# Attention scores that VectorE writes from PSUM into the probabilities' tiles, with new instruction orders for three engines

## The chip, the core and the metric

The kernel runs on one core of one Trainium2 chip. A core has TensorE (PE in the profile; its weight loads are listed apart as PEld), VectorE (DVE), ScalarE (ACT), GpSimd (POOL) and the queue SyncE (SP), which here only issues transfers. The metric is the device time of one execution in microseconds, the median over several.

## The reference

One layer of a streaming encoder on 1024 frames of width 1024, all in float32: a norm and one wide projection; eight heads of "forgetting" attention; eight heads of attention in a band; both mixed under gates; an output projection; a feed-forward block; a last norm. The change lies in the attention:

```
# forgetting heads: causal, the logits get the summed log forget gates
sc = einsum('bhqd,bhkd->bhqk', qi, k) * scale + ci[..., None] - c[:, :, None, :]
sc = where(key_pos <= tq, sc, NEG)
# band heads: own chunk of 64 and the eight before it, and a bias by distance
sc = where(valid, einsum('bhqd,bhkd->bhqk', qi, kb) * scale + bias, NEG)
# both
p = softmax(sc); out = einsum('bhqk,bhkd->bhqd', p, v)
```

## The kernel before

Everything outside the attention is dense products in units of a Strassen scheme: float32 operands are split into a high and a low half, and each product is three matmuls of 128 rows by 512 columns. Around the attention, a gate projection runs ahead of it and the rest of the branch products behind it.

The 16 heads are worked off one after the other, the eight forgetting heads first (`HEADS`, pairs 4 to 7), then the eight band heads. A head has eight blocks of 128 queries. Block i of a forgetting head meets i+1 blocks of keys, so 36 in all; in a band head at most five, so 30. The steps of a head have letters:

- S (`make_scores`, `score`): TensorE makes a block's scores, in two terms (operand `qk` of 128 rows, `sk` of 96), in a PSUM tile `s` of 1024 columns. There are two such tiles.
- R (`take_lowest`, `lowest`): VectorE adds the mask (`wide`) or the band's bias (`bc`), takes the negative, writes that back over the scores, and takes each row's minimum into `mn`; a second, short instruction reads the minimum out.
- E (`take_exp`, `soften`): ScalarE makes the exponential of the negative with `mn` as bias, which gives the probabilities `p`, and their sum in `den`. There is one tile `p` for each block index (tag `p0` to `p7`), so a head overwrites those of the head before.
- T (`turn`): TensorE transposes blocks of `p` into a PSUM tile `pt`, in groups of up to four (`key_groups`). A forgetting head has ten groups: three for the first four query blocks, seven for the last four. It rotates over three PSUM tiles, a band head over two.
- H (`round_p`): ScalarE rounds `pt` to the high half `th`. L (`low_p`): VectorE makes the rest, `tl`. Four tiles of each.
- P (`weigh_next`): TensorE multiplies `th` and `tl` with the values into one PSUM tile `pv`, for each half of the queries.
- V and X (`evacuate`, `evacuate_rest`): ScalarE, and for the second half VectorE, take `pv` out (`on`, `lo`, `mv`).
- F: a step of the branch product, three matmuls, as filling for TensorE in band heads from the tenth head on (`FILL_FROM = 9`); M takes its result out. W and O are weights and outputs for the branch product at the end.

The order is written out by hand. The strings `INTRO`, `FOX_HEAD`, `BAND_HEAD` and `LAST_HEAD` list the letters of a head; each engine keeps the order of its own letters (`Ordered`). T, H, L, P of a string belong to its own head, S, R, E to the head after it, since eight chunks of S, R and E are done ahead, between the steps of the last gate projection. `INTRO` is issued first and its letters are then taken out of the first string. A scheduler places the rest, outside of the attention, by itself.

A step waits for its data and for its buffer: S for the scores' tile of two chunks before, T for its `pt` tile, H and L for their tiles, the first P of a half for `pv`. Line 106 is the helper that issues every ordered instruction, so nearly all rows of the attention carry L106, and tiles tell them apart.

Of the kernel before, what the change touches and what calls it, by code (L numbers as in the profile page):

```python
# [18 lines left out]
P = 128  # L19
# [8 lines left out]
BAND = 640  # L28
# [10 lines left out]

HEADS = [(pr, hh) for pr in (4, 5, 6, 7, 0, 1, 2, 3) for hh in range(2)]  # L40
SK = HD + 32
INTRO = "TTTHHLHLPTHPLTLHPVTTH"
FOX_HEAD = "STTHRSETSHLRLREPTHLPTHESHLPVTRTELSRXHTLHSPEPHLTPTSHRLPEPHLRLESPRPVXE"
BAND_HEAD = "TTFSRHEFFHSLLFSMTHRPTPELFTFPRHLEHSVTLSFRXTHRPPELSTFHLERPHLESMPRPVESRXE"
LAST_HEAD = "FFFFMWTHTFFFLHFTPLTWPHMLFFWFFTHHLMLTPFFHLTVFXFHLPPMOOTHLOPPOPWVXOO"
FILL_FROM = 9

LEAD, XB, XR = 3, 4, 6

# [43 lines left out]
def hybrid_block(ctx: ExitStack, tc: tile.TileContext, xT, xN, g1, wall, wf, fb, relb, g2, g3, outT):  # L93
# [17 lines left out]
    def pool(stack, name, side, bufs=1, **kw):  # L111
        return stack.enter_context(tc.tile_pool(name=name, bufs=bufs, side=side, reuse_waits="tile", **kw))
# [366 lines left out]
    def load_head(n, eng):  # L479

        pr, hh = HEADS[n]
        e, p = 2 * pr + hh, apq[n % 2]
        qk = p.tile([P, 2, S], F32R, tag="qk", name=f"qk{n}")
        if n < 2:
            sks.append(p.tile([SK, 2, S], F32R, tag="sk", name=f"sk{n}"))
            G.memset(sks[n][HD:SK].bitcast(F32), 0.0)
            G.memset(sks[n][HD:HD + 3, 1, :].bitcast(F32), -1.0)
        sk = sks[n % 2]
        if pr >= 4:
            loads.append(eng.dma_start(sk[HD:HD + 3, 0, :].bitcast(F32), c3_dram[:, 2 * (pr - 4) + hh, :]).ins)  # L490
        elif n < 10:
            G.memset(sk[HD:SK, 0, :].bitcast(F32), 0.0)
        loads.append(eng.dma_start(qk.bitcast(F32), qk_dram[e]).ins)
        loads.append(eng.dma_start(sk[0:HD].bitcast(F32), sk_dram[e]).ins)
        operands[n] = (qk, sk)

    loads, sks, biases, operands, smalls, probs = [], [], {}, {}, {}, {}

    def score(n, i, bank, te):

        pr = HEADS[n][0]
        qk, sk = operands[n]
        j0, W = window(pr, i)
        off = P if W == BAND else 0
        spans = [(max(off, HALF * x), min(off + W, HALF * (x + 1))) for x in range(2 if off + W > HALF else 1)]
        rows = slice(i * P, (i + 1) * P)
        for t, w in enumerate((qk, sk)):
            for a, b in spans:
                keys = slice(j0 * P + a - off, j0 * P + b - off)
                te.matmul(bank[:, a:b], w[:, 1, rows], w[:, 0, keys], start=t == 0, stop=t == 1)  # L510

    def lowest(n, i, bank, ve):

        pr = HEADS[n][0]
# [151 lines left out]
    apq = [pool(astack, "apq0", "right")]  # L666
    app = pool(astack, "app", "right")
    load_head(0, G)
    chunks = [(n, i) for n in range(16) for i in range(8)]
    made, cut, spent = [], [], []  # L670

    def make_scores():
        if len(made) == len(chunks):
            return
        n, i = chunks[len(made)]
        made.append(pss.tile([P, S], F32, tag="s", name="s"))
        score(n, i, made[-1], TO)
        if i == 7 and 0 < n < 14:
            load_head(n + 2, LO)

    def take_lowest(ve=VO):
        if len(cut) < len(chunks):
            n, i = chunks[len(cut)]
            lowest(n, i, made[len(cut)], ve)
            cut.append(None)
            if i == 7 and n + 2 < 16:
                load_bias(n + 2, LO)

    def take_exp(ae=AO):
        if len(spent) < len(chunks):  # L690
            soften(*chunks[len(spent)], made[len(spent)], ae)
# [259 lines left out]
    def branch_weight():  # L951
# [6 lines left out]
        G.tensor_tensor(wl, raw, wh.bitcast(F32), op=ALU.subtract)  # L958

    acts = {"O": split_o, "W": branch_weight, "S": make_scores, "R": take_lowest, "E": take_exp, "T": turn, "H": round_p, "L": low_p, "P": weigh_next,  # L960
            "V": evacuate, "X": evacuate_rest, "F": filler, "M": gate_fill}
    heads = [t for n, (pr, hh) in enumerate(HEADS) for t in
             (FOX_HEAD if pr >= 4 else LAST_HEAD if n == 15 else BAND_HEAD if n >= FILL_FROM else
              BAND_HEAD.replace("F", "").replace("M", ""))]
    for t in INTRO:
        heads.remove(t)
    for t in chain(INTRO, heads):
        acts[t]()
        if t == "S" and len(made) in (8 * FILL_FROM - 4, 8 * FILL_FROM):
            next(fills)  # L970
# [376 lines left out]
```

## Time and profile before

| | us |
|---|---|
| median of 3 runs (lowest, highest) | 1427.55 (1426.97, 1428.85) |
| profiled execution | 1430.48 |
| its span, first to last instruction | 1428.5 |
| mean granted TensorE clock in it | 0.995 |
| attention, about | 400 to 665 of the span |

The span begins after some 2 us that belong to the execution and not to the profile. Times in rows of the trace count from the span's start. A group's row gives busy time, mean ns of one instruction, and the idle time before them with what ended it. In the view by windows each stretch lists its length, then PE, PEld, DVE, ACT and POOL busy with their numbers of instructions, the granted clock, the DMA share and GB/s.

### The profile page before, as it was taken

Reading aid. Unit: us, or ns where it says so; the run is one execution under the profiler, and the core shown is the slowest. Engines: PE = TensorE matmul, PEld = TensorE weight load, DVE = VectorE, ACT = ScalarE, POOL = GpSimd, SP = SyncE. Lnnn points to the kernel's source line nnn. Section 1 sums busy time; section 2 is a strip of 40 time slices with the busy share of each in tenths; the row PEclk is TensorE's granted clock in tenths of the full one; section 3 lists DMA queues with packets and bytes.
Section 4 is the critical chain, followed back from the end, with each engine's and each line's share of the span. In section 5 each row is a group of like instructions: output and inputs, shape, how many; then the busy total and the mean of one; then the engine's idle time right before and its main releaser. Section 6 shows DMA issues by size and latency. Waiting matters only on the chain.

```text
span 1428.5 us, 20411 instructions
## 1 busy us (share of the span) xinstructions
PE 1400.7 (98%) x6676; PEld 1168.7 (82%) x6676; DVE 885.1 (62%) x1389; ACT 706.6 (49%) x1361; POOL 812.2 (57%) x639
## 2 busy tenths in 40 slices
PE   9999999999999999999999999999999999999996
PEld 6788888888878888888888888888888888888885
DVE  7756445543258887776655855545555559998644
ACT  8534333343358887775454543333333444444653
POOL 0477777778832233113724677777777545567564
PEclk9999999999999999999999999999999999999998
DMA  8546667773454668886644244444444784678263
GB/s 282 154 116 194 187 196 219 204 198 121 147 169 147 185 209 248 246 257 215 213 162 146 68 166 151 155 154 157 148 154 169 252 269 156 178 234 225 81 221 118
DMA packets 132820, 259.75 MB, mean 182 GB/s; under 512 B 18594, under 2 KB 20642, under 8 KB 129642
## 3 DMA queue, kind: packets, MB, share of 16 engines
q1 hardware_dynamic: 84570, 172.79, 38.6%
q10 hardware_dynamic: 44944, 77.78, 17.2%
q0 software_dynamic: 3200, 7.88, 2.5%
q8 instruction: 52, 0.85, 0.2%
q14 instruction: 54, 0.44, 0.1%
HBM read 172.70 MB, written 85.69 MB: 181 GB/s over the span
## 4 chain that ended last, share of the span: by engine, by line
PE 87%; DVE 3%; issue 3%; ACT 2%; POOL 2%; DMA 2%; SPq 0%; POOLq 0%; ACTq 0%; DVEq 0%
PE u L216 44%; PE dS L216 12%; PE dA L216 5%; PE o L216 5%; PE s L106 5%; PE pv L106 4%; PE pt L106 3%; PE m L106 3%; PE m L216 3%; POOL wl_A L165 1%; PE u L106 1%; DMA xg<-xT 1%; DMA xT<-a_dram 1%; ACT p L106 1%; PE vtp L627 0%
## 5 line engine op out<-in xcount | busy, mean ns | idle before, releaser
L165 POOL TENSOR_TENSOR wl_A<-wr,wh_A 128x512 fp32r<-128x512 f32 x118 | 158.4, 1352 | 94.0 <-ACT wh_A L163 77.0
L165 POOL TENSOR_TENSOR wl_S<-S,wh_S 128x512 fp32r<-128x512 f32 x102 | 136.0, 1337 | 32.9 <-ACT wh_S L163 32.3
L163 ACT CAST wh_S<-S 128x512 fp32r<-128x512 f32 x105 | 64.6, 621 | 114.0 <-PE u L216 53.9
L163 ACT CAST wh_A<-wr 128x512 fp32r<-128x512 f32 x105 | 65.0, 620 | 88.7 <-PE u L216 55.8
L106 DVE TENSOR_TENSOR tl<-pt,th 128x512 fp32r<-128x512 f32 (+1 forms) x144 | 90.5, 641 | 25.9 <-ACT th L106 24.4
L165 POOL TENSOR_TENSOR wl_S<-ks,wh_S 128x512 fp32r<-128x512 f32 x48 | 69.1, 1501 | 53.4 <-ACT wh_S L106 50.0
L590 DVE TENSOR_TENSOR u<-u,u 128x512 f32<-128x512 f32 x70 | 48.8, 698 | 76.0 <-PE u L216 73.6
L106 ACT ACTIVATE p<-s,mn 128x640 f32<-128x640 f32 (+3 forms) x120 | 84.4, 703 | 16.6 <-DVE mn L106 15.5
L106 ACT CAST th<-pt 128x512 fp32r<-128x512 f32 (+1 forms) x144 | 77.6, 551 | 24.5 <-PE pt L106 22.3
L106 PE MATMUL pt<-ident,p 128*128 128x128 f32 x528 | 78.1, 274 | 1.2 <-DVE zt L403 1.1
L186 POOL TENSOR_TENSOR S<-wr,wr 128x512 f32<-128x512 f32 x35 | 46.3, 1324 | 54.8 <-DMA wr<-wall 50.2
L106 PEld LDWEIGHTS pt<-ident,p 128*128 128x128 f32 x528 | 62.2, 141 | 11.0 <-PE pv L106 2.0
L106 PE MATMUL s<-qk 128*128 128x384 f32 (+2 forms) x192 | 58.6, 360 | 8.1 <-ACT p L106 7.3
L165 POOL TENSOR_TENSOR wl_A<-ka,wh_A 128x512 fp32r<-128x512 f32 x32 | 45.1, 1419 | 35.6 <-ACT wh_A L106 34.1
L278 ACT CAST qkh<-qk 128x512 fp32r<-128x512 f32 x32 | 19.9, 621 | 87.5 <-DMA qk_dram<-qkl 34.2
L1102 ACT ACTIVATE v<-v 128x512 f32<-128x512 f32 x64 | 40.4, 632 | 45.1 <-DVE v L1101 42.9
L924 POOL TENSOR_TENSOR on<-on,lo 128x512 f32<-128x512 f32 x7 | 9.0, 1292 | 92.7 <-ACT lo L106 92.7
L106 PE MATMUL pv<-th,v 128*128 128x512 f32 (+3 forms) x180 | 61.3, 348 | 0.1
L583 DVE TENSOR_TENSOR u<-u,c 128x512 f32<-128x512 f32 x35 | 24.5, 699 | 59.4 <-PE u L216 57.3
L106 PE MATMUL pv<-tl,v 128*128 128x512 f32 (+3 forms) x180 | 56.8, 335 | 0.2 <-DVE tl L106 0.2
L1101 DVE SCALAR_TENSOR_TENSOR v<-u,rstd 128x512 f32<-128x512 f32 x64 | 43.9, 688 | 20.1 <-PE u L216 18.1
L581 DVE TENSOR_TENSOR c<-u,u 128x512 f32<-128x512 f32 x35 | 24.2, 691 | 50.7 <-PE u L216 48.9
(445 smaller groups left out, 4742.2 us busy)
## 6 DMA issues: line engine op xcount, KB each, us to landing
wr<-wall SPq DMA_DIRECT2D x233, 256.0 KB
a_dram<-at ACTq DMA_DIRECT2D x64, 256.0 KB
xT<-a_dram SPq DMA_DIRECT2D x64, 256.0 KB
qk<-qk_dram SPq DMA_DIRECT2D x15, 1024.0 KB
qk_dram<-qkh ACTq DMA_DIRECT2D x96, 128.0 KB
a_dram<-v ACTq DMA_DIRECT2D x48, 256.0 KB
xB<-a_dram SPq DMA_DIRECT2D x44, 256.0 KB
z_dram<-zt ACTq DMA_DIRECT2D x32, 256.0 KB
```

What stands on the lines that cost most here:

```text
L106: return lambda *a, **kw: tc.keep_in_program_order(getattr(self.eng, name)(*a, **kw))
L163: (act.tensor_copy if act is G or act is V else act.copy)(wh, src)
L165: lows.append(eng.tensor_tensor(wl, src, wh.bitcast(F32), op=ALU.subtract))
L186: eng.tensor_tensor(t, raw(3), raw(2), op=ALU.add)
L216: done = eng.matmul(bank, w[wi], x[xi], start=(first and t == 0), stop=(t == n - 1 and not part), skip_group_check=part or not first)
L278: A.copy(dst[0], src)
L581: V.tensor_tensor(c22, banks[2], u2, op=ALU.add)
L583: V.tensor_tensor(banks[1], banks[3], c22, op=ALU.add)
L590: V.tensor_tensor(banks[b], banks[b], u2, op=ALU.add)
L924: G.tensor_tensor(o, o, lows_o[pr], op=ALU.add)
L1101: V.scalar_tensor_tensor(v, src, 0.0, rstd[:, hs(h)], op0=ALU.max, op1=ALU.mult)
L1102: A.activation(v, v, AF.Square)
```

## The change

The minimum step writes the shifted scores into the probabilities' tile `p` in SBUF instead of back into PSUM, and the exponential works in place there. The PSUM tile `s` is so read by VectorE alone, and the tile `p` is taken by `lowest` instead of `soften`. The blocks of a head go in the order 0 to 5, 7, 6 instead of 0 to 7. The four strings are new; each has the same letters of each kind as before, save that `INTRO` now holds 24 letters instead of 21 (eight T instead of seven, two S and one R, which were not in it, one L more, one P less and no V).

```diff
-INTRO = "TTTHHLHLPTHPLTLHPVTTH"
-FOX_HEAD = "STTHRSETSHLRLREPTHLPTHESHLPVTRTELSRXHTLHSPEPHLTPTSHRLPEPHLRLESPRPVXE"
...
+INTRO = "TTTHHLTLHHLPTHLPLTTSSRHT"
+FOX_HEAD = "TTHHSSRSTRHLSLEPLTRETHHPLLPTVHRSTXLTSPRTHLSTRPEEHLREHEPSHLPLPPPREVXE"
...
+FOX_BLOCKS = (0, 1, 2, 3, 4, 5, 7, 6)
+BAND_BLOCKS = (0, 1, 2, 3, 4, 5, 7, 6)
...
         x = bank[:, off:off + W]
+        p = probs[n, i] = app.tile([P, (i + 1) * P], F32, tag=f"p{i}", name=f"p{n}_{i}")
         more = wide[:, S - W:S] if pr >= 4 else biases[n][:, BAND - W:BAND]
-        ve.tensor_tensor_reduce(x, x, more, -1.0, 3.0e38, ALU.add, ALU.min, smalls[n][:, i:i + 1])
+        ve.tensor_tensor_reduce(p[:, :W], x, more, -1.0, 3.0e38, ALU.add, ALU.min, smalls[n][:, i:i + 1])
...
-    def soften(n, i, bank, ae):
+    def soften(n, i, ae):
...
-        p = probs[n, i] = app.tile([P, (i + 1) * P], F32, tag=f"p{i}", name=f"p{n}_{i}")
+        p = probs[n, i][:, :W]
...
-            ae.activation(p[:, :W], bank[:, off:off + W], AF.Exp, scale=-1.0, bias=smalls[n][:, i:i + 1],
+            ae.activation(p, p, AF.Exp, scale=-1.0, bias=smalls[n][:, i:i + 1],
                          accum_out=smalls["den", pr][:, 8 * hh + i:8 * hh + i + 1])
...
-    chunks = [(n, i) for n in range(16) for i in range(8)]
+    chunks = [(n, i) for n, (pr, hh) in enumerate(HEADS) for i in row_blocks(pr)]
```

The first place is ScalarE at the boundary of two forgetting heads. `mv` is the copy of the old head's last `pv`; the casts to `th` after it are the first of the new head. Before:

```order
L106 ACTIVATE p_6_4479,den_4330<-s,mn_4325 128x896
L106 COPY mv_1_4499<-pv 64x512
L106 ACTIVATE p_7_4505,den_4330<-s,mn_4325 128x1024
L106 CAST th<-pt 128x512
L106 ACTIVATE p_0_4530,den_4330<-s,mn_4525 128x128
L106 CAST th<-pt 128x512
L106 ACTIVATE p_1_4545,den_4330<-s,mn_4525 128x256
L106 CAST th<-pt 128x256
```

With the change:

```order
L113 ACTIVATE p_7_4466,den_4348<-p_7_4466,mn_4329 128x1024
L113 COPY mv_1_4500<-pv 64x512
L113 ACTIVATE p_6_4497,den_4348<-p_6_4497,mn_4329 128x896
L113 CAST th<-pt 128x512 x2
L113 CAST th<-pt 128x256
L113 ACTIVATE p_0_4530,den_4348<-p_0_4530,mn_4529 128x128
L113 ACTIVATE p_1_4540,den_4348<-p_1_4540,mn_4529 128x256
```

The exponentials read `p` instead of `s`; block 6 is the one that stands behind `mv`; the first three casts of the new head stand ahead of its exponentials of blocks 0 and 1, which lay between them.

The second place is TensorE at the same kind of boundary, up to the first value matmul (`pv`) of the new head. Before:

```order
L106 MATMUL s<-qk_4118 128x128
L106 MATMUL s<-sk_3810 128x128
L106 MATMUL pt<-ident,p_0_4201 128x128
...
L106 MATMUL pt<-ident,p_3_4216 128x128 x2
L106 MATMUL s<-qk_4118 128x256
L106 MATMUL s<-sk_3810 128x256
L106 MATMUL pt<-ident,p_2_4210 128x128
L106 MATMUL pt<-ident,p_3_4216 128x128
L106 MATMUL s<-qk_4118 128x384
L106 MATMUL s<-sk_3810 128x384
L106 MATMUL pv<-th,v_4122 128x512
```

With the change:

```order
L113 MATMUL pt<-ident,p_3_4222 128x128 x2
L113 MATMUL s<-qk_4118 128x128
L113 MATMUL s<-sk_3810 128x128
L113 MATMUL s<-qk_4118 128x256
L113 MATMUL s<-sk_3810 128x256
L113 MATMUL s<-qk_4118 128x384
L113 MATMUL s<-sk_3810 128x384
L113 MATMUL pt<-ident,p_2_4214 128x128
L113 MATMUL pt<-ident,p_3_4222 128x128
L113 MATMUL s<-qk_4118 128x512
L113 MATMUL s<-sk_3810 128x512
L113 MATMUL pv<-th,v_4122 128x512
```

The first two groups of transposes stand ahead of all scores, the scores of blocks 0 to 2 follow each other, and those of block 3 (512 columns) stand ahead of the first `pv` too.

The third place is VectorE there; `ISA` is the minimum, with its read-out in a row of its own behind it. With the change it reads:

```order
L113 TENSOR_TENSOR tl<-pt,th 128x256
L113 ISA p_6_4300,mn_4194<-s,wide 128x896
L113 ISA mn_4194 128x1
L113 TENSOR_TENSOR on_1_4297<-pv,mv_1_4303 64x512
L113 ISA p_0_4330,mn_4329<-s,wide 128x128
L113 ISA mn_4329 128x1
L113 ISA p_1_4340,mn_4329<-s,wide 128x256
L113 ISA mn_4329 128x1
L113 TENSOR_TENSOR tl<-pt,th 128x512 x2
```

Before, the first `tl` of a head stood between the minima of blocks 0 and 1; now it stands behind both, and the last minimum of a head (block 6) behind its last `tl`.

More of the change, by code (lines that the diff above doesn't have):

```diff
@@ L41 @@
 SK = HD + 32
-INTRO = "TTTHHLHLPTHPLTLHPVTTH"
-FOX_HEAD = "STTHRSETSHLRLREPTHLPTHESHLPVTRTELSRXHTLHSPEPHLTPTSHRLPEPHLRLESPRPVXE"
-BAND_HEAD = "TTFSRHEFFHSLLFSMTHRPTPELFTFPRHLEHSVTLSFRXTHRPPELSTFHLERPHLESMPRPVESRXE"
-LAST_HEAD = "FFFFMWTHTFFFLHFTPLTWPHMLFFWFFTHHLMLTPFFHLTVFXFHLPPMOOTHLOPPOPWVXOO"
+INTRO = "TTTHHLTLHHLPTHLPLTTSSRHT"
+FOX_HEAD = "TTHHSSRSTRHLSLEPLTRETHHPLLPTVHRSTXLTSPRTHLSTRPEEHLREHEPSHLPLPPPREVXE"
+BAND_HEAD = "THSFSRTFHFREFSLSLTPRTPHHLPRVTSHMFLTLFSXHPTELHRPTPEHFLSERLEPFERSPMREVXE"
+LAST_HEAD = "THFWFLFFTTMPFWFHLFFTPHLPMTHHLLFFFFMTWTHVLPFFXWHTHFLFPLMPPOOPOOVXOO"
 FILL_FROM = 9
+FOX_BLOCKS = (0, 1, 2, 3, 4, 5, 7, 6)
+BAND_BLOCKS = (0, 1, 2, 3, 4, 5, 7, 6)
 LEAD, XB, XR = 3, 4, 6
@@ L73, in window, with row_blocks @@
     return j0, (i + 1 - j0) * P
+def row_blocks(pr):
+    return FOX_BLOCKS if pr >= 4 else BAND_BLOCKS
 def key_groups(pr, h):
@@ L516, in lowest @@
         off = P if W == BAND else 0
-        if i == 0:
+        if n not in smalls:
             smalls[n] = aps.tile([P, 8], F32, tag=f"mn{n % 2}", name=f"mn{n}")
         x = bank[:, off:off + W]
+        p = probs[n, i] = app.tile([P, (i + 1) * P], F32, tag=f"p{i}", name=f"p{n}_{i}")
         more = wide[:, S - W:S] if pr >= 4 else biases[n][:, BAND - W:BAND]
-        ve.tensor_tensor_reduce(x, x, more, -1.0, 3.0e38, ALU.add, ALU.min, smalls[n][:, i:i + 1])
-    def soften(n, i, bank, ae):
+        ve.tensor_tensor_reduce(p[:, :W], x, more, -1.0, 3.0e38, ALU.add, ALU.min, smalls[n][:, i:i + 1])
+    def soften(n, i, ae):
         pr, hh = HEADS[n]
         W = window(pr, i)[1]
-        off = P if W == BAND else 0
-        if i == 0 and hh == 0:
+        p = probs[n, i][:, :W]
+        if ("den", pr) not in smalls:
             smalls["den", pr] = aps.tile([P, 16], F32, tag="den", name=f"den{pr}", bufs=2)
-        p = probs[n, i] = app.tile([P, (i + 1) * P], F32, tag=f"p{i}", name=f"p{n}_{i}")
         with tc.issue_after(sigmoids[-1]):
-            ae.activation(p[:, :W], bank[:, off:off + W], AF.Exp, scale=-1.0, bias=smalls[n][:, i:i + 1],
+            ae.activation(p, p, AF.Exp, scale=-1.0, bias=smalls[n][:, i:i + 1],
                          accum_out=smalls["den", pr][:, 8 * hh + i:8 * hh + i + 1])
@@ L677, in make_scores @@
         score(n, i, made[-1], TO)
-        if i == 7 and 0 < n < 14:
+        if len(made) % 8 == 0 and 0 < n < 14:
             load_head(n + 2, LO)
@@ L685, in take_lowest @@
             cut.append(None)
-            if i == 7 and n + 2 < 16:
+            if len(cut) % 8 == 0 and n + 2 < 16:
                 load_bias(n + 2, LO)
@@ L690, in take_exp @@
         if len(spent) < len(chunks):
-            soften(*chunks[len(spent)], made[len(spent)], ae)
+            soften(*chunks[len(spent)], ae)
             spent.append(None)
```

## The prediction

> **What bounds the kernel now.** I read the page's busy line first, then the stretch of the attention with the view by windows, then who waits there, then the instructions in order of time at three places.
>
> ```profile
> PE 1400.7 (98%) x6676; PEld 1168.7 (82%) x6676; DVE 885.1 (62%) x1389; ACT 706.6 (49%) x1361; POOL 812.2 (57%) x639
> core 0: us, PE busy (x) PEld busy (x) DVE busy (x) ACT busy (x) POOL busy (x), PEclk, DMA share, GB/s
> 417.90:430.87 12.97, 9.95 (x55) 8.05 (x54) 8.27 (x19) 8.38 (x21) 0.00 (x0) 0.87 0.60 178
> 473.34:487.62 14.28, 13.60 (x85) 11.54 (x85) 12.54 (x28) 12.70 (x31) 7.13 (x7) 1.00 0.64 185
> 562.93:579.28 16.35, 16.35 (x104) 14.71 (x104) 12.40 (x28) 11.83 (x28) 3.79 (x3) 1.00 0.91 291
> ```
>
> TensorE bounds the whole, but its 98% is a modelled figure, so I count its work instead. The chain of waits gives the pitch, and the marks of two heads:
>
> ```profile
> 430.87 0.24 PE pv L106
> 442.36 0.87 PE pt L106 x8
> 444.96 0.93 PE pv L106 x4
> 530.00 0.93 PE pv L106 x4
> ```
>
> A transpose takes 0.87/8 = 0.109 us, a matmul of 512 columns 0.93/4 = 0.233, so 0.058 for each block of 128. From 430.87 to 530.00 are seven forgetting heads: 14.16 us each. Such a head has 36 blocks: 36 x 0.109 for the transposes, 72 x 0.058 for the scores (two terms each), 72 x 0.058 for the values: 3.92 + 4.18 + 4.18 = 12.3 us. How far can TensorE get to that? The band head with filling (562.93 to 579.28) has 30 blocks and 24 filling matmuls: 3.27 + 3.48 + 3.48 + 5.58 = 15.8, and took 16.35 without a wait of PE; so 0.54 per head go into changes of shape. The floor of a forgetting head is thus 12.8, and 1.35 us per head are real waits. Between 430.87 and 516, for six heads, the waits are:
>
> ```profile
> PE s L106 <- ACT p L106: 3.9, 6, 0.8
> PEld s L106 <- ACT p L106: 7.9, 15, 1.1
> ACT p L106 <- DVE mn L106: 7.5, 12, 1.0
> ```
>
> 7.9 of the 8.1 us that six heads lose: the scores wait for a PSUM tile that the exponential has not yet read. ScalarE and VectorE are busy for 12.7 and 12.5 of 14.3, so they are close behind. At the boundary of two heads, in order of time:
>
> ```profile
> 450.40 0.28 PE L106 MATMUL pv<-tl,v 128*128 128x256 f32 x1
> 450.71 0.58 ACT L106 COPY mv<-pv 64x512 f32<-64x512 f32 x1
> 451.32 1.11 ACT L106 ACTIVATE p<-s,mn 128x1024 f32<-128x1024 f32 x1
> 452.42 0.58 ACT L106 CAST th<-pt 128x512 fp32r<-128x512 f32 x1
> 452.57 0.19 PEld L106 LDWEIGHTS s<-qk 128*128 128x128 f32 x1 [0.81 <-ACT p L106]
> 453.03 0.69 DVE L106 TENSOR_TENSOR tl<-pt,th 128x512 fp32r<-128x512 f32 x1 [0.58 <-ACT th L106]
> 453.41 0.19 PEld L106 LDWEIGHTS s<-qk 128*128 128x128 f32 x1 [0.35 <-ACT p L106]
> 453.87 0.40 PE L106 MATMUL pv<-th,v 128*128 128x512 f32 x1
> ```
>
> The copy `mv` waits for the last value matmul, the exponential of block 7 for the copy, and the second scores of the next head for that exponential (0.81), the third for the one after (0.35).
>
> **The change, part by part.** *The bank.* The score tile is read by VectorE alone now, so scores wait for the minimum two chunks back, not for its exponential. That takes an exponential (up to 1.11 us) and the queue before it on ScalarE out of the loop over two tiles; the 1.3 us per head go, as far as nothing else is late.
>
> *What is late next.* The probabilities' tile is now written by the minimum, which so has to wait for the last transposes of the same block of the head before; what stands behind it on VectorE are the low parts `tl`, for which the value matmuls wait. The new order meets this: the minima of blocks 0 and 1 stand ahead of the first `tl`, those of 7 and 6 behind the last transposes. I followed the new rows once round with the durations above. Within a head all waits are met, the tightest by 0.2 us (the scores of block 5 on the minimum of block 3, the last but one value group on its `tl`). What stays is the boundary: last value matmul, 0.31 to `mv`, about 0.5 for it, 1.0 for the exponential of block 6 (1.11 in the row of block 7, which is an eighth larger), then the first `th`, 0.61 to `tl`, and 0.5 to the value matmul (0.84 in the rows above, less the scores that stood between). That is 2.95 us from the last value matmul's start, 2.8 from its end. In this time PE has ten transposes (1.09) and the scores of ten blocks (1.16, and 0.3 for four changes): 2.55. So about 0.3 of waiting is left: 12.8 + 0.3 = 13.1, and I take 13.2, with 0.1 for what one round does not show. Seven heads x (14.16 - 13.2) = **6.7 us**.
>
> *Costs that the trace does not show.* An exponential from SBUF and a minimum into SBUF do not occur; the nearest rows are:
>
> ```profile
> L577 ACT COPY p<-u 128x512 f32<-128x512 f32 x35 | 20.3, 581 | 1.3 <-PE u L216 1.3
> L163 ACT CAST wh_A<-wr 128x512 fp32r<-128x512 f32 x105 | 65.0, 620 | 88.7 <-PE u L216 55.8 <-DMA a_dram<-at 30.5 <-DVE fc L459 1.4
> L590 DVE TENSOR_TENSOR u<-u,u 128x512 f32<-128x512 f32 x70 | 48.8, 698 | 76.0 <-PE u L216 73.6 <-PE u L106 2.3
> L581 DVE TENSOR_TENSOR c<-u,u 128x512 f32<-128x512 f32 x35 | 24.2, 691 | 50.7 <-PE u L216 48.9 <-PE u L106 1.3
> L1109 DVE TENSOR_TENSOR at<-v,at 128x512 f32<-128x512 f32 x32 | 35.5, 1111 | 21.4 <-ACT v L1102 21.3
> ```
>
> ScalarE from PSUM 581 ns, from SBUF 620: +0.04 for each exponential; one of eight lies on the boundary, 0.04 per head, and is in the 13.2 (below: nothing; above: all eight, 0.3 per head). VectorE from PSUM and SBUF into PSUM 698, into SBUF 691: nothing, as the new minimum has just the operands of the 691 row. The other end is the row with all operands in SBUF, 1111; I take 691, since one operand stays in PSUM.
>
> The Trainium skill's page Perfetto Trace Analysis (Optimizing Scalar/DVE Operations) puts the fixed part of a VectorE operation at about 60 ns on SBUF and 125 on PSUM. By it the eight minima would be up to 0.5 us per head shorter; the two rows differ by 7 ns for the output side, so I count nothing. If the page held here too, the rival in which VectorE is late (the first below) would lose a part of its chance.
>
> *The start.* From the first transposes to the first value matmul of the second half:
>
> ```profile
> 417.71 0.60 PE L106 MATMUL pt<-ident,p 128*128 128x128 f32 x4
> 419.39 0.87 PE L106 MATMUL pt<-ident,p 128*128 128x128 f32 x6 [1.08 <-DVE zt L403]
> 420.36 1.62 DVE L106 TENSOR_TENSOR tl<-pt,th 128x512 fp32r<-128x512 f32 x3 [1.02 <-ACT th L106]
> 425.28 0.44 PE L106 MATMUL s<-qk 128*128 128x384 f32 x1 [0.69 <-ACT p L106]
> 427.42 0.90 PE L106 MATMUL s<-qk 128*128 128x384 f32 x2 [0.91 <-ACT p L106]
> 430.70 0.40 PE L106 MATMUL pv<-th,v 128*128 128x512 f32 x1
> 428.00:430.00 2.00, 2.00 (x10) 1.90 (x9) 0.99 (x3) 1.19 (x5) 0.00 (x0) 0.50 0.69 260
> ```
>
> The first two steps stay (they wait for the gates' banks). Then the waits of 0.69 and 0.91 on exponentials fall away, the transposes are issued one group earlier, and the scores stand where a `tl` is awaited anyhow. Following the new rows: fourth transposes at 421.1, scores from 423.8, scores of block 5 at 426.4, value matmul at 427.4, not 430.7: **3.3 us**. Half of that hangs on the granted clock. It fell to 0.50 in 428 to 430 after waits of at most 1.08 us each, and the work from 427.42 to 430.70 (scores of 11 blocks, four transposes: 1.28 + 0.44 = 1.7 us) took 3.3. If the remaining waits (1.2 and 1.0 us at 418 and 420) do the same, 1.7 us are won.
>
> The Trainium skill's page TensorE: Matmul & The Clock Gate (What's actually happening) has the array throttled after an idle window of some 3.4 us. No single wait here is that long, and the clock fell all the same, so the trace disagrees; by the page the new start would not be throttled, and the 3.3 would be safe.
>
> *The band heads.* Six of them are filled: 16.35 us without a wait of PE, and the same instructions stay, so nothing changes. The cover there is 5.6 us of filling per head: gone with it would be the boundary's 0.4. The ninth head, the first band head, has no filling:
>
> ```profile
> 535.26 0.87 PE pt L106 x8
> 536.28 0.89 ACT p L106 x2
> 548.24 0.77 PE pt L106 x7
> ```
>
> It takes 13.0 us for 3.27 + 6.96 + 0.54 = 10.8 of work. In the new order one wait is in sight: the fourth scores behind the minimum of block 1, which waits for the second transposes, 0.4. So 11.2: **1.8 us**. The last head and all behind it have their instructions unchanged and start earlier; SP's loads stand in nearly the same order, keyed to the same steps.
>
> The sum: 6.7 + 3.3 + 1.8 = **11.8 us**. It is made against the profiled execution, 1428.5 of span and 1430.48 in all. The median of the runs is 1427.55, 3 below; I take the difference off that: 1415.8, **1416**.
>
> **Rivals.** Three rows for them:
>
> ```profile
> 446.18 1.09 ACT L106 CAST th<-pt 128x512 fp32r<-128x512 f32 x2
> L106 DVE CUSTOM_DVE_ANT_0 s<-s,wide 128x1024 f32<-128x1024 f32 x2 | 2.5, 1233 | 0.4 <-PE s L106 0.2
> L106 DVE CUSTOM_DVE_ANT_0 s<-s,wide 128x128 f32<-128x128 f32 x2 | 0.6, 290 | 0.0
> ```
>
> *Half of it*: ScalarE or VectorE, busy for 12.7 and 12.5 now, cannot be packed into 13.2 with 0.3 more on ScalarE, and small waits on `th` and `tl` come back on PE. For it: 0.2 us of slack at the tightest places. Against: their busy times overlap, since two `th` in a row take 1.09, not twice 0.58. A head would take 13.7: 7 x 0.46 + 1.7 + 1.0 = 5.9, that is 1421.5.
> *The wait only moves*: the minimum has to wait for the transposes just as long as the scores waited for the exponential, so that the tile is free no earlier. Against: the transposes of blocks 0 to 3 come first in a head. Then only part of the start is won: 1426.
> *Slower*: the minimum runs at the price of the row with all operands in SBUF, 1111/691 = 1.6 times as long. The eight minima of a head, 128 to 1024 wide, take 8 x (0.29 + 1.23)/2 = 6.1 us: +3.7 on VectorE's 12.5 makes 16.2, above 14.16. It decides from +1.7 us per head on. Eight heads x 2.0 = 16, less 3 at the start and nothing in the filled heads: about 1440; at half the surcharge VectorE needs 14.3 and the loss in the heads is about what the start wins: 1427.
>
> **How the numbers follow.** The forecast, 1411.5 to 1419.5, has 0.66: its lower end is the floor of 12.8 in all heads (7 x 1.35 + 3.3 + 2.2 = 15), its upper end the throttled start and 13.4 per head. Half of it has 0.20, the moved wait 0.08, slower 0.06. The range for 8 in 10 is 1411.5 to 1422. About 0.2%, 2.9 us, can be told from no change here; below 1424.7 lie the first two cases: faster 0.86, same 0.08, slower 0.06.
>
> **What would show it.** Right: "PE s <- ACT p" is gone from the waits; heads follow each other at 13.0 to 13.4 us; the first value matmul of the second half lies at about 427.5 with the clock at 1.00 before it; the filled heads stay at 16.35; exponentials are 0.04 longer, minima unchanged. Wrong: "PE s <- DVE mn" in the place of the old wait, minima of 512 columns well above 0.70, a filled head with PE waits, or a half clock at the start.

## The result and the profile after

| | before | after |
|---|---|---|
| median of the runs (lowest, highest), us | 1428.20 (1426.97, 1429.68), 4 runs | 1420.74 (1419.68, 1422.30), 4 runs |
| profiled execution, its span, us | 1430.48, 1428.5 | 1421.05, 1419.3 |
| ratio, 95% interval | | 0.9944 (0.9932 to 0.9956) |

The kernel became faster by 0.56%, about 7.5 us. The forecast was 1416, with 1411.5 to 1422 as its wider range: 1420.74 lies inside that, but above the 1411.5 to 1419.5 of the main case. The direction and the mechanism came out, and the gain is about two thirds of the 11.8 us that were summed up.

Where the 9.2 us between the two spans come from, read at five marks: the first transposes of the attention, the copies `mv` of the first and of the eighth head (one `mv` closes each of these heads), the first product of the branch stage behind the attention, and the first one-column product of the second norm. The marks of the changed kernel, from its instructions in order of time:

```profile
417.82 0.60 PE L113 MATMUL pt<-ident,p 128*128 128x128 f32 x4
433.31 0.58 ACT L113 COPY mv<-pv 64x512 f32<-64x512 f32 x1
526.62 0.58 ACT L113 COPY mv<-pv 64x512 f32<-64x512 f32 x1
655.26 0.91 PE L223 MATMUL m<-oh,wh_ab 128*128 128x512 f32 x3
796.35 0.28 PE L273 MATMUL n_s<-ones,rstd 128*128 128x1 f32 x2
```

Before, these marks lie at 417.71, 436.44, 535.68, 664.88 and 805.96; the middle three:

```profile
436.44 0.58 ACT L106 COPY mv<-pv 64x512 f32<-64x512 f32 x1 [0.37 <-PE pv L106]
535.68 0.58 ACT L106 COPY mv<-pv 64x512 f32<-64x512 f32 x1
664.88 0.45 PE L216 MATMUL m<-oh,wh_ab 128*128 128x512 f32 x1
```

By differences:

| stretch, us | before | after | gain | forecast |
|---|---|---|---|---|
| start: first transposes to first `mv` | 18.73 | 15.49 | 3.24 | 3.3 |
| seven heads: first to eighth `mv` | 99.24 | 93.31 | 5.93 (0.85 a head) | 6.7 (0.96 a head) |
| band heads: eighth `mv` to the branch stage | 129.20 | 128.64 | 0.56 | 1.8 |
| branch stage to second norm | 141.08 | 141.09 | 0.0 | 0 |
| second norm to the end | 622.5 | 622.95 | -0.4 | 0 |

Now the heads. The waits of TensorE and its weight loads over seven heads (433 to 527) in the changed kernel; columns are the total, the number and the longest:

```profile
PEld s L113 <- DVE mn L113: 3.8, 7, 0.6
PE s L113 <- DVE mn L113: 2.4, 7, 0.4
PEld pv L113 <- DVE tl L113: 2.1, 8, 0.3
```

"PE s <- ACT p" and "PEld s <- ACT p", which the forecast showed with 3.9 and 7.9 us in six heads, are gone. What is left are two short waits at each boundary of two heads, and none inside a head but two of the weight loads at the end of the eighth (0.16 and 0.27). One such boundary of the changed kernel, in order of time:

```profile
473.02 0.29 PE L113 MATMUL pv<-tl,v 128*128 128x256 f32 x1
473.35 0.58 ACT L113 COPY mv<-pv 64x512 f32<-64x512 f32 x1 [0.25 <-PE pv L113]
473.95 1.04 ACT L113 ACTIVATE p<-p,mn 128x896 f32<-128x896 f32 x1
473.96 0.69 DVE L113 TENSOR_TENSOR on<-pv,mv 64x512 f32<-64x512 f32 x1 [0.54 <-ACT mv L113]
474.69 0.29 DVE L113 CUSTOM_DVE_ANT_0 p<-s,wide 128x128 f32<-128x128 f32 x1
474.90 0.42 DVE L113 CUSTOM_DVE_ANT_0 p<-s,wide 128x256 f32<-128x256 f32 x1
474.99 1.36 ACT L113 CAST th<-pt 128x512 fp32r<-128x512 f32 x3
475.04 0.44 PE L113 MATMUL s<-qk 128*128 128x384 f32 x1 [0.40 <-DVE mn L113]
475.59 1.62 DVE L113 TENSOR_TENSOR tl<-pt,th 128x512 fp32r<-128x512 f32 x3 [0.26 <-ACT th L113]
476.33 0.19 PEld L113 LDWEIGHTS pv<-tl,v 128*128 128x128 f32 x1 [0.18 <-DVE tl L113]
```

Two chains leave from `mv`. ScalarE's: `mv`, the exponential of block 6, `th`, then `tl`. VectorE's: `mv`, the addition `on`, the minima of blocks 0 and 1, then `tl`. The first is the one that the forecast walked. The second makes the scores of block 2 wait 0.40 (their PSUM tile is free once block 0 has its minimum), and reaches `tl` only 0.26 earlier than the first.

Unit prices in the attention of the changed kernel (groups kept apart by shape: count, busy time, mean ns of one):

```profile
L113 ACT ACTIVATE p<-p,mn 128x512 f32<-128x512 f32 x15 | 10.8, 723 | 0.0
L113 DVE CUSTOM_DVE_ANT_0 p<-s,wide 128x512 f32<-128x512 f32 x7 | 4.8, 682 | 0.0
L113 DVE DVE_READ_ACCUMULATOR2_ANT mn<- 128x1 f32 x120 | 9.9, 83 | 0.0
```

Before, in the same view, the three took 690, 699 and 138 ns; the last:

```profile
L106 DVE DVE_READ_ACCUMULATOR2_ANT mn<- 128x1 f32 x120 | 16.5, 138 | 0.2
```

The exponential from SBUF is 0.03 longer; the minimum is 0.02 shorter and its read-out 0.055 shorter. VectorE is busy for 12.0 us of a head instead of 12.5.

The clock at the start, and the tenth head:

```profile
424.00:428.00 4.00, 4.00 (x26) 3.46 (x25) 3.35 (x13) 3.19 (x9) 0.00 (x0) 1.00 0.39 133
521.01 2.74 SPq L113 DMA_DIRECT2D r_dram<-rt  x4
527.66 1.10 SPq L113 DMA_DIRECT2D rb<-r_dram  x2
528.85 0.54 SPq L113 DMA_DIRECT2D qk<-qk_dram  x1
529.48 0.45 SPq L113 DMA_DIRECT2D sk<-sk_dram  x1
526.00:530.00 4.00, 3.47 (x22) 2.58 (x22) 3.57 (x11) 3.37 (x10) 0.78 (x1) 1.00 0.27 72
530.00:534.00 4.00, 4.00 (x30) 3.77 (x29) 2.91 (x8) 3.22 (x7) 1.49 (x2) 1.00 1.02 326
539.23 0.33 PE L113 MATMUL s<-sk 96*128 96x128 f32 x1 [0.44 <-DMA sk<-sk_dram]
542.31 0.29 DVE L113 CUSTOM_DVE_ANT_0 p<-s,bc 128x128 f32<-128x128 f32 x1 [1.45 <-DMA bc<-relb]
```

The rows with a colon are the view by windows, with granted clock, DMA share and GB/s at their ends; "SPq" are SP's issues. The clock stays at 1.00 at the start. But in the tenth head PE waits for `sk` and VectorE for the band's bias `bc`, which the forecast did not have. On SP's queue `rb` (the reciprocals, spread out) waits until the store `r_dram` of the same data has landed; this store stands behind 1.5 MB for the filling (two `wrab`, four `z`). While SP stands there, the DMA engines run dry (share 0.27 from 526 to 530), and behind it `qk` and `sk` of a later head come out late and land late. SP's own wait there:

```profile
SPq L113 <- DMA r_dram<-rt: 3.6, 1, 3.6
```

### The profile page after: what moved, and what is told of

It is laid out like the page before. It is cut to its first block, busy times and chain, and to the rows that moved or that the text cites. A ratio compares the mean times of both kernels' runs of the same rounds, so it can differ in the third digit from the quotient of the medians.

```text
span 1419.3 us, 20288 instructions
## 1 busy us (share of the span) xinstructions
PE 1396.9 (98%) x6676; PEld 1168.7 (82%) x6676; DVE 884.0 (62%) x1389; ACT 707.8 (50%) x1361; POOL 811.9 (57%) x639
## 4 chain that ended last, share of the span: by engine, by line
PE 86%; DVE 4%; issue 3%; POOL 2%; DMA 2%; ACT 1%; POOLq 0%; ACTq 0%; SPq 0%; DVEq 0%
PE u L223 42%; PE dS L223 12%; PE dA L223 7%; PE o L223 5%; PE s L113 4%; PE pv L113 4%; PE pt L113 3%; PE m L113 3%; PE m L223 3%; POOL wl_A L172 1%; PE u L113 1%; DMA wr<-wall 1%; DMA sk<-sk_dram 1%; DMA xg<-xT 1%; DVE xg L337 1%
## 5 line engine op out<-in xcount | busy, mean ns | idle before, releaser
L113 ACT ACTIVATE p<-p,mn 128x640 f32<-128x640 f32 (+3 forms) x120 | 87.8, 736 | 0.7 <-DVE mn L113 0.4
L172 POOL TENSOR_TENSOR wl_A<-ka,wh_A 128x512 fp32r<-128x512 f32 x32 | 45.2, 1422 | 36.3 <-ACT wh_A L113 34.9
L223 PE MATMUL u<-B11h,wh_A 128*128 128x512 f32 x140 | 55.3, 395 | 0.2 <-DVE vs L286 0.2
```

Source lines behind the costliest of these rows:

```text
L113: return lambda *a, **kw: tc.keep_in_program_order(getattr(self.eng, name)(*a, **kw))
L172: lows.append(eng.tensor_tensor(wl, src, wh.bitcast(F32), op=ALU.subtract))
L223: done = eng.matmul(bank, w[wi], x[xi], start=(first and t == 0), stop=(t == n - 1 and not part), skip_group_check=part or not first)
```

## Experiments

Each ran beside the kernel before. The stretches come from the marks above in the profiled execution of each; "pitch" is the mean of the seven heads, "band" the stretch from the eighth `mv` to the branch stage, the tenth head is from the ninth `mv` to the tenth. The old and the new strings put this `mv` at different places in the work of the band heads, so the column of the tenth head compares runs with the new strings; ninth and tenth head together take 28.28 before and 27.97 in e2. The versions e9 and e10 leave out the values' low halves in 384 of 512 columns, and so do not compute the reference; they are there to measure.

| run | median, us | ratio (95%) | start | pitch | tenth head | band |
|---|---|---|---|---|---|---|
| before, first profile | | | 18.73 | 14.18 | 16.32 | 129.20 |
| after, first profile | 1420.74 | 0.9944 (0.9932 to 0.9956) | 15.49 | 13.33 | 15.83 | 128.64 |
| e1 bank only | 1427.88 | 0.9995 (0.9987 to 1.0003) | 18.13 | 14.08 | 16.34 | 129.01 |
| e2 early fetch | 1419.40 | 0.9929 (0.9917 to 0.9941) | 15.46 | 13.32 | 15.12 | 127.33 |
| e3 minimum first | 1425.11 | 0.9970 (0.9958 to 0.9981) | 15.46 | 13.47 | 21.49 | 133.69 |
| e4 exponential later | 1421.96 | 0.9952 (0.9937 to 0.9967) | 17.07 | 13.23 | 18.90 | 131.00 |
| e5 after, again | 1422.32 | 0.9950 (0.9937 to 0.9963) | 15.46 | 13.33 | 16.89 | 129.10 |
| e6 e4 + e2 | 1419.24 | 0.9932 (0.9920 to 0.9944) | 15.46 | 13.23 | 15.83 | 128.42 |
| e7 e3 + e2 | 1420.43 | 0.9941 (0.9929 to 0.9953) | 15.46 | 13.47 | 16.87 | 129.07 |
| e8 blocks 0 to 7 + e2 | 1420.05 | 0.9938 (0.9926 to 0.9949) | 15.45 | 13.45 | 15.12 | 127.34 |
| e9 short `on` + e2 | 1420.41 | 0.9943 (0.9929 to 0.9958) | 17.02 | 13.37 | 15.17 | 127.27 |
| e10 short `on` + e4 + e2 | 1416.86 | 0.9922 (0.9905 to 0.9939) | 15.47 | 13.00 | 15.17 | 126.75 |
| e11 old INTRO + e2 | 1421.00 | 0.9947 (0.9932 to 0.9962) | 15.98 | 13.33 | 15.12 | 127.84 |
| e12 fetch earlier still | 1422.84 | 0.9948 (0.9929 to 0.9967) | 17.04 | 13.60 | 15.12 | 127.32 |

### The bank alone (e1)

```diff
-INTRO = "TTTHHLTLHHLPTHLPLTTSSRHT"      (and the other three new strings)
+INTRO = "TTTHHLHLPTHPLTLHPVTTH"         (and the other three of before)
-FOX_BLOCKS = (0, 1, 2, 3, 4, 5, 7, 6)
+FOX_BLOCKS = tuple(range(8))            (BAND_BLOCKS too)
```

> Only the freed bank: the minimum writes p in SBUF and the exponential works in place there, but the four strings and the block order 0 to 7 are those of before. Theory (the bank frees the scores, the new order meets the waits that follow): the scores no longer wait for an exponential, but they stand in the row where the old order put them, and the casts of a new head still stand behind and between exponentials, so waits on tl and on the minimum take the place of a part: 13.6 to 13.9 us for a forgetting head (14.16 before, 13.34 with the whole change), total 1423 to 1425. Rival (the bank is all, the order nothing): 13.34 and 1420.7. Rival (the wait only moves without the order): 14.1 and 1427.

It gained nothing that can be measured: 0.9995 (0.9987 to 1.0003), and 14.08 us a head against 14.18. The 13.6 to 13.9 of the theory was missed; this is the outcome of the rival in which the wait only moves, as long as the order is the old one. Its waits over six heads (436 to 522):

```profile
PEld pv L113 <- DVE tl L113: 3.2, 6, 0.5
PEld s L113 <- DVE mn L113: 2.6, 6, 0.7
PEld pv L113 <- ACT th L113: 2.2, 5, 0.5
ACT p L113 <- DVE mn L113: 7.8, 13, 0.9
```

The scores wait no longer for an exponential, but the value matmuls now wait for `tl` and `th`, which stand behind the same exponentials and minima as before. So the freed bank is a permission: what it permits is the new order. The new order alone was not run, since it has no way through with the old bank: its third scores stand on TensorE ahead of the third transposes, they would wait for the exponential of block 0, which stands on ScalarE behind the third cast, which waits for those transposes. That follows from the strings; no run shows it. What the order does with the bank freed is shown by the other runs: 14.08 here, 13.45 with the new strings and the old order of blocks (e8), 13.33 with all.

### Which chain holds the boundary (e3, e4, e6, e7, e9, e10)

The strings around a boundary of heads, with "|" between them:

```diff
-...PPPREVXE|TTHHSSRSTRHLSLE...
+...PPPREVE|TTHHSSRXSTRHLSLE...     e3, e7: X behind the first R
+...PPPREVX|TTHHESSRSTRHLSLE...     e4, e6: E behind the second H
```

> The changed kernel with one move on VectorE at each boundary of heads (up to the filled ones): the minimum of block 0 ahead of the evacuation on<-pv,mv. Theory (two chains of nearly the same length end at the first value matmul of a head: scores of block 2 on the minimum behind on, and tl behind mv, exponential of block 6 and th): the wait of the scores on mn, 0.4 per head, goes, and pv waits for tl by that much longer: 13.3 per head, total unchanged within 0.5 (1420.5). Rival (what the trace names as releaser, the minimum behind on, is all): 0.4 x 8 = 3.2 lower, 1417.5.

> The changed kernel with one move on ScalarE at each boundary of heads (up to the filled ones): the exponential of block 6 behind the first two casts th of the new head instead of ahead of them. Theory (two chains): tl comes 1.0 earlier and PE's wait on it, 0.18 to 0.3 per head, goes; the scores' wait of 0.4 on the minimum behind on stays: 13.1 to 13.2 per head, total 1419 to 1419.8. Rival (the chain through the exponential is all): 0.5 per head, 12.8, total 1416.5. Rival (ScalarE, busy 12.8 of 13.3, is the bound): nothing, 1420.7.

e4 came out close to what the two chains give for a head: 13.23, where 13.1 to 13.2 was expected, and 12.8 or 13.33 by the rivals. Its total did not get better, for two other reasons (below): in its profile, 1.6 us of lowered clock at the start and 3.1 us of late loads in the tenth head. e3 made a head longer, 13.47, which neither theory had said. At one boundary of e3:

```profile
460.72 0.29 DVE L113 CUSTOM_DVE_ANT_0 p<-s,wide 128x128 f32<-128x128 f32 x1 [0.96 <-PE s L113]
460.93 0.68 DVE L113 TENSOR_TENSOR on<-pv,mv 64x512 f32<-64x512 f32 x1
462.00 0.19 PEld L113 LDWEIGHTS s<-qk 128*128 128x128 f32 x1 [0.33 <-DVE mn L113]
```

VectorE idles for 0.96 until the scores of block 0 are there, with `on` and the minimum of block 1 queued behind. The move cost more on VectorE than it took away, so it could not separate the chains. For that VectorE's chain has to be made shorter instead of rearranged: `on` for 128 columns instead of 512, which leaves out a part of the result, alone and with the later exponential, both with the early fetch (e2, below) so that late loads disturb less.

```diff
-VO.tensor_tensor(outs[pr, h][rows], pv[rows], moved.pop((n, h))[rows], op=ALU.add)
+o, mv, w = outs[pr, h], moved.pop((n, h)), P if n < 8 else HALF
+VO.tensor_tensor(o[rows, 0:w], pv[rows, 0:w], mv[rows, 0:w], op=ALU.add)
+if w < HALF:
+    G.tensor_copy(o[rows, w:], mv[rows, w:])
```

> With the early fetch, the evacuation on<-pv,mv of the second halves of the eight forgetting heads made by VectorE for 128 of 512 columns only (GpSimd copies mv for the others, so the values' low halves are left out there): about 0.4 less on VectorE at each boundary. Theory (two chains end at the first value matmul: VectorE's mv, on, two minima, tl, and ScalarE's mv, exponential, th, then tl): the scores' wait of 0.4 on the minimum goes, but tl still waits for th, so the heads stay at 13.3, at most 0.05 shorter. Rival (VectorE's chain alone is the bound): 13.0, 2.5 us below the early fetch.

> The short evacuation (values' low halves left out in 384 of 512 columns of the second halves) and the later exponential together, with the early fetch. Theory (two chains): each alone gives 0.0 to 0.1, both together take both chains away: 12.85 to 12.95 per head, 3 us below the early fetch, ratio 0.9905. Rival (ScalarE, busy 12.8 of 13.3, or something else inside the head is the bound): 13.15 or more, ratio 0.9925.

The four pitches make a square: neither move 13.32 (e2), ScalarE's alone 13.23 (e6), VectorE's alone 13.37 (e9), both 13.00 (e10). Alone they bring 0.09 and less than nothing, together 0.32: two chains of nearly equal length that end at the same place. The waits show it too. In e9 the wait of PE on the minimum is gone, and that on `tl` has grown from 2.1 to 4.0 over the same eight boundaries (430 to 530):

```profile
PEld pv L113 <- DVE tl L113: 4.0, 8, 0.5
PEld s L113 <- DVE mn L113: 2.4, 8, 0.3
```

In e10 TensorE itself no longer waits on either: what is left are waits of weight loads, which run beside the matmuls, and TensorE is the bound. A head of e10 by windows (length, then PE, PEld, DVE, ACT, POOL busy with counts, clock, DMA share, GB/s), and its waits:

```profile
472.65:485.66 13.01, 12.90 (x87) 11.59 (x86) 11.60 (x29) 12.44 (x29) 6.91 (x7) 1.00 0.65 164
PEld s L113 <- DVE mn L113: 2.4, 8, 0.3
PEld pv L113 <- DVE tl L113: 0.3, 1, 0.3
```

12.90 of 13.01 is TensorE's own work, so the floor is 12.9 to 13.0 and not 12.8 as estimated (a busy time of TensorE is modelled, the pitch of 13.00 is not). The pitch lies 0.05 above the expected 12.85 to 12.95, and the total, 0.9922 (0.9905 to 0.9939), has the expected 0.9905 only at its end. ScalarE and VectorE, 12.4 and 11.6 busy, do not bound a head of 13.0.

### What is late in the tenth head (e2, e5, e6, e7, e12)

```diff
-if t == "S" and len(made) in (8 * FILL_FROM - 4, 8 * FILL_FROM):
+if t == "S" and len(made) in (8 * FILL_FROM - 12, 8 * FILL_FROM):     e2, e6 to e11
+if t == "S" and len(made) in (8 * FILL_FROM - 20, 8 * FILL_FROM):     e12
```

> The changed kernel with the first fetch of the filling (two wrab and four z loads, 1.5 MB, on SP's queue) issued eight chunks earlier, at the same chunk of the head before. Theory (qk and sk of the eleventh head come late because they stand on SP's queue behind rb, which waits for the r_dram store, which the 1.5 MB delays): the wait of 9.70 us from issue to landing of sk and PE's waits at 539 to 543 (sk 0.44, bc on VectorE 1.45) go, the stretch from the end of head 9 to the branch stage falls from 117.3 to about 116.4, total 0.9 lower, 1419.8. Rival (the DMA engines are simply full there, 530 to 550 at 1.0): the same bytes come late elsewhere, total unchanged within 0.3.

> The changed kernel itself, beside the three that follow, to compare with the early fetch and to see what differs between two executions of one program. Theory: 7 to 9 us below the kernel before (0.9935 to 0.9955); tenth head 15.8 us again if its late loads belong to the program, 15.1 if the delay was chance; the granted clock at the second norm, 0.50 for 6 us in the first profile, is chance and may be 1.00.

> The two moves together: exponential of block 6 behind two casts, and the filling's first fetch eight chunks earlier. Theory (the run with the later exponential lost 3 us in its tenth head, 18.9 against 15.8, to loads that landed later still, and won 0.1 in each head before): tenth head 15.1, heads 13.2; 0.7 to 1.0 below the early fetch alone, ratio 0.992 to 0.9925. Rival (the later exponential itself costs in the band heads): tenth head above 17, ratio 0.994 or more.

> The two moves together: minimum of block 0 ahead of the evacuation, and the early fetch. Theory (of the 3.7 us by which the earlier minimum was slower than the changed kernel, 1.1 come from heads of 13.37 and 13.63 instead of 13.34, because VectorE waits 0.96 for the scores with the evacuation behind it, and the rest is the tenth head, 21.5 instead of 15.8): tenth head 15.1, heads 13.5, 1.0 to 1.3 above the early fetch alone, ratio 0.9937. Rival (the tenth head's loss hangs on the minimum, not on the loads): ratio 0.996 or more.

> The filling's first fetch 16 chunks earlier than in the changed kernel (the early fetch: 8). Theory (what is late in the tenth head are loads behind 1.5 MB and an r_dram store on SP's queue, by different amounts from execution to execution: 15.8, 16.9, 18.9, 21.5 without, 15.1, 15.8, 16.9, 15.1 with the early fetch): 15.1 again, ratio 0.992 to 0.993, no different from the early fetch. Rival (the rest of the loads is late by itself): 15.8 to 16.9.

With the fetch eight chunks earlier the tenth head took 15.12, the waits for `sk` and `bc` were gone, and the band stretch fell by 1.31 to 127.33, where 0.9 was expected. The DMA engines then work where they idled in the changed kernel:

```profile
526.00:530.00 4.00, 3.53 (x25) 2.71 (x24) 3.58 (x12) 3.22 (x8) 3.22 (x4) 1.00 1.04 323
```

They still idle, but earlier (share 0.10 from 520 to 522), and SP still waits for the store, 3.3 us in all against 3.6. So the move does not shorten that wait. It lets SP reach the store sooner: the store's first issue stands 9.2 us ahead of the eighth `mv` in e2, 5.6 in the changed kernel, and 9.2 in the kernel before, where the fetch stood behind it.

How late the loads are differs between programs that issue them at nearly the same time, and between two executions of one program: the tenth head took 15.83 and 16.89 in the changed kernel, 18.90 in e4 and 21.49 in e3, whose loads of `qk` were issued at 529.4 and 528.9, the changed kernel's at 528.85. In e3:

```profile
542.91 0.48 PE L113 MATMUL s<-sk 96*128 96x128 f32 x1 [2.79 <-DMA sk<-sk_dram]
546.43 0.29 DVE L113 CUSTOM_DVE_ANT_0 p<-s,bc 128x128 f32<-128x128 f32 x1 [5.25 <-DMA bc<-relb]
```

Not all of e3's 21.49 is waiting for loads. In that wait of 2.79 us the granted clock fell, and it stayed at 0.50 until 548:

```profile
542.00:546.00 4.00, 3.08 (x11) 2.80 (x12) 0.00 (x0) 0.35 (x1) 1.26 (x1) 0.50 1.02 253
```

In e4, which waited 2.50 us for `sk`, it stayed at 1.00. From the end of this wait to the tenth `mv` e3 took 18.4 us and e4 16.3, so about 2 us of e3 are the clock. With the early fetch e7 has the boundary of e3 and a tenth head of 16.87, and its ratio is 0.9941 instead of 0.9970: most of what e3 lost was the loads and what followed from them. The fetch lowers the delay and does not always end it: 15.12 or 15.17 in five of the seven profiles that have it at this place, 15.83 in e6 and 16.87 in e7, where SP waited 4.9 and 4.7 us for the store; but in e8 it waited 4.7 as well, with 15.12. Moved earlier still (e12), it stands again directly ahead of an `r_dram` store, that of the pair before, and the same thing happens two heads sooner. The issues of e12 and VectorE's wait in the first band head's scores:

```profile
495.81 3.27 SPq L113 DMA_DIRECT2D r_dram<-rt  x4
502.31 1.09 SPq L113 DMA_DIRECT2D rb<-r_dram  x2
505.25 1.54 SPq L113 DMA_DIRECT2D bc<-relb  x2
519.23 0.29 DVE L113 CUSTOM_DVE_ANT_0 p<-s,bc 128x128 f32<-128x128 f32 x1 [1.92 <-DMA bc<-relb]
```

The tenth head is at 15.12 there, and the head before the first band head at 15.15 instead of 13.3. The expectation for the tenth head held, that for the total did not. So the largest delays go with the place: loads that stand on SP's queue behind an `rb` whose `r_dram` store stands directly behind the 1.5 MB. What is left of them in e6 and e7, and why the same loads take different times from one execution to the next, stays open.

Against the changed kernel, the early fetch is at 0.9929 (0.9917 to 0.9941) where that is at 0.9944 and 0.9950. The intervals overlap, so the times alone do not show a gain over the changed kernel; the profiles have 1.3 to 1.8 us in the band stretch for it. Against the kernel before the gain is clear, and the ratio is the lowest of the versions that compute the whole reference; e6, which has a head 0.1 shorter, is level with it and not the expected 0.7 to 1.0 below.

### The order of blocks and the start (e8, e11)

```diff
-FOX_BLOCKS = (0, 1, 2, 3, 4, 5, 7, 6)                  e8
+FOX_BLOCKS = tuple(range(8))                           (BAND_BLOCKS too)
-INTRO = "TTTHHLTLHHLPTHLPLTTSSRHT"                     e11
+INTRO = "TTTHHLHLPTHPLTLHPVTTH"
```

> With the early fetch, the blocks of a head in the order 0 to 7 again, so that block 7 and not block 6 has its exponential behind mv and its minimum last in a head. Theory (the boundary is the bound: VectorE's and ScalarE's chains from mv to the first value matmul): 0.13 us longer minimum and exponential at the boundary, up to 0.15 per head, 1.2 us above the early fetch alone. Rival (it makes no difference): within 0.3 of it.

> With the early fetch, the first string (INTRO) of before again, the rest new. Theory (the start wins by its own order: the first value matmuls stood ahead of transposes whose results they need, and the bank alone gave 0.6 there): first transposes to mv of the first head 17.5 to 18.5 us instead of 15.5, heads 13.34 as before, 2 to 3 us above the early fetch alone. Rival (the start's gain comes from the bank and the clock): 15.5 to 16.5 and less than 1 us.

e8: 13.45 a head against 13.32, by the 0.13 expected: the larger block's exponential (1161 ns against 1043 in the changed kernel) and minimum on the boundary's chains. So the exchange of blocks 6 and 7 is worth about 0.9 us over seven heads; the medians differ by 0.65, inside their noise.

e11: the start took 15.98 against 15.46. The rival holds for the start: the new `INTRO` itself is worth 0.5. Its median lies 1.6 above e2, more than the rival's 1, but the intervals of the two ratios overlap. An estimate of the 3.2 us that the start won, from these rows: 0.6 by the bank (18.73 to 18.13), 1.6 by the granted clock (18.13 to about 16.5, if the fall cost e1 as much as the three profiles below), 0.5 by the strings behind it (to 15.98) and 0.5 by `INTRO` (to 15.46). With the new `INTRO`, eight of eleven profiles have 15.45 to 15.49 there, and three (e4, e9, e12) 17.02 to 17.07. Two windows of e4, to be laid beside the row of the changed kernel above:

```profile
420.00:424.00 4.00, 3.40 (x16) 3.10 (x17) 2.62 (x5) 1.76 (x4) 0.00 (x0) 0.65 0.98 274
424.00:428.00 4.00, 4.00 (x27) 3.68 (x26) 2.49 (x10) 2.42 (x7) 0.00 (x0) 0.92 0.48 149
```

The instructions and waits before are the same (1.08 us, then 0.83, with nothing but transposes between them); in these three the clock fell, and that costs 1.6 us. Before, and in e1, the clock had fallen in the one profile of each; in e11, with the old `INTRO`, it had not.

## Why the prediction was right, and where it was not

- **What bounds the kernel.** Right: the scores' wait on the exponential bounded the heads, and it is gone. The 7.9 us that were set against 8.1 are waits of weight loads, though; those of the matmuls themselves were 3.9. The floor of a head was put at 12.8; e10 shows 12.9 to 13.0, so the waits of a head before were 1.2 to 1.3 us and not 1.35.
- **"The 1.3 us per head go, as far as nothing else is late."** The condition carried nearly all of it. The bank alone gives 0.1 per head (e1); the rest needs the order as well. The forecast followed both together and did not say that the bank alone would give next to nothing.
- **The boundary, 13.2 per head.** Mechanism right, size off: 13.33. The walk took ScalarE's chain (`mv`, exponential, `th`, `tl`) and left 0.3 of waiting. In the trace the weight loads wait 0.18 to 0.35 for `tl` at each boundary, and VectorE's chain beside it, which the forecast did not walk, makes the scores wait another 0.40 for the minimum behind `on`. Seven times 0.13 is 0.9 us, less 0.15 since the mark `mv` puts a head of before at 14.18 and not 14.16. Inside a head no wait is left, as forecast; the tightest places with 0.2 us of slack held.
- **Prices.** The exponential from SBUF, +0.04 taken, +0.03 measured. The minimum was counted as unchanged; with its read-out it is 0.07 shorter, 0.6 per head for eight minima. The Trainium skill's page Perfetto Trace Analysis (Optimizing Scalar/DVE Operations), with some 60 ns of fixed cost on SBUF and 125 on PSUM, gave 0.5 per head: the trace agrees with it in the sum, but not in the place. The minimum itself is only 17 ns shorter; the rest is in the read-out (138 to 83 ns), which the rows quoted in the forecast could not show. The rival "slower", a minimum 1.6 times as long, has nothing left for it.
- **The start, 3.3.** 3.24 in the profiles, with the value matmul at 427.54 where 427.4 was forecast. "Half of that hangs on the granted clock" was right as well, and that this half came out in the profile was luck: 1.6 us are lost again in three of the eleven profiles with the new `INTRO`.
- **The ninth head, 1.8.** Off in two ways, and the total hides one. The band stretch falls from 129.20 to 127.33 when the loads are in time (e2), by 1.9 us, but not in the ninth head alone. By the marks of the forecast, first transposes to first transposes, the ninth head went from 13.0 to 11.7 and not to 11.2, a gain of 1.3; in the changed kernel:

```profile
526.43 0.60 PE L113 MATMUL pt<-ident,p 128*128 128x128 f32 x4
538.10 0.62 PE L113 MATMUL pt<-ident,p 128*128 128x128 f32 x4
```

  The rest comes from where the forecast had nothing: 0.4 from the six filled heads (16.29 instead of 16.35 each) and 0.6 from the last head, whose string is new. (The three make 2.2 or 2.3 and not 1.9, because the eighth `mv` lay 0.6 us behind the ninth head's first transposes before and lies 0.2 behind them now.) In the changed kernel only 0.56 and 0.1 (two profiles) are kept of it all. The step that failed there is "SP's loads stand in nearly the same order, keyed to the same steps": the steps come earlier, and the fetch of 1.5 MB, which stood behind an `r_dram` store, now stands ahead of it, so that the store and everything behind it on SP is late. The loads on SP were never walked along with the three engines.
- **Everything behind only earlier.** Right up to the second norm (141.08 and 141.09). There the clock fell in both first profiles, and for longer in that of the changed kernel; this row is of that place:

```profile
802.00:806.00 4.00, 4.00 (x11) 3.09 (x11) 3.09 (x16) 1.15 (x3) 2.82 (x3) 0.52 0.05 18
```

  From the mark of the second norm to the next transposes (`n_b`) took 12.98 us before and 14.54 after, so 1.6 us were taken back. Of these 1.1 were gone by the end, 0.7 of it by a wait of TensorE on GpSimd near the end (0.74 at 1407) that the profile of before has and that of after has not. The second profile of the changed kernel (e5) has 12.95 here: its clock fell for a shorter time. It fell in seven of the fourteen profiles, and not in e3, e4, e6 to e8, e11 and e12. It does not belong to the change.
- **The sum.** 11.8 = 6.7 + 3.3 + 1.8; measured 9.7 = 5.9 + 3.2 + 0.6 to the end of the attention, and 7.5 and 7.1 between the medians of the two timings. A part of the difference between the two is that the profiled execution of before is 2.3 us above its median, that of after 0.3: the forecast took a sum that held 1.6 us of a lowered clock off a median that need not hold them.
- **The signs.** Three signs of being right came as forecast: the old wait is gone, heads follow at 13.33, and the value matmul lies at 427.54 with the clock at 1.00. But two signs of being wrong came as well. "PE s <- DVE mn" is there, though with 2.4 us in seven heads it is smaller than the 3.9 in six that it replaces; that is VectorE's chain at the boundary. And the tenth head, a filled one, has a wait of PE (0.44 on `sk`).
- **The rivals.** The time, 1420.74, lies nearest to "half of it" (1421.5), but not for its reason: ScalarE and VectorE could be packed into 13.33, and no small waits came back inside the heads. "The wait only moves" is what happens with the bank alone.

## What to carry to other kernels

A buffer that was freed earlier gave nothing by itself here, with engines that keep a written order: the same order found its next wait (0.9995); ask what order it permits, and cost that. At the seam of two loops walk the chain of every engine that starts from the same event, not only the one you know: two chains of equal length hide each other, and only taking both away shows it (0.09, nothing, 0.32). When a total comes out near its forecast, split it by the forecast's own terms: the 1.9 us of the band heads looked like the 1.8 of the ninth head and were not. And when work moves earlier, walk the DMA queue too: a load that had to wait 3.6 us for a store to land stopped everything queued behind it.

## What the runs showed of the hardware

- The granted clock falls to 0.50 for some microseconds in some executions and not in others that run the same instructions there. At the start it showed 0.65 from 420 to 424 in e4 and 1.00 in the changed kernel, both after waits of 1.08 and 0.83 us among transposes. At the second norm, around 16 matmuls of one column with one wait of 0.8, it fell in seven of fourteen profiles, in the changed kernel's two for different lengths. In the tenth head it fell in a wait of 2.79 us (e3) and not in one of 2.50 (e4). The Trainium skill's page TensorE: Matmul & The Clock Gate (What's actually happening) asks for an idle window of some 3.4 us; no single wait at any of these places is that long.
- The read-out of VectorE's accumulator takes 83 ns behind a minimum that writes into SBUF, 138 behind one that writes into PSUM; the scores are read from PSUM in both.
- Loads issued within 1 us of each other in four executions landed up to 4 us apart (`sk` let PE go at 539.2 in the changed kernel, at 542.9 in e3), at a DMA share of about 1.0 in both and with 288 and 179 GB/s moved from 538 to 542.
